# A gate product in blocks of two, and sums made by adding transfers, in a two-layer hybrid backbone

## The chip, the cores and the metric

The kernel runs on one core of one Trainium2 chip. The metric is the device time of one execution in microseconds. Engines are called as in the profile: PE (TensorE, the matmuls), DVE (VectorE), ACT (ScalarE), POOL (GpSimd), SP (SyncE, which here only issues transfers).

## What is computed

Two layers over 1024 latent tokens of width 1024, and 256 context tokens. Layer 0 has a convolution branch A and a recurrent branch B behind one input projection; layer 1 is a pooling mixer. Everything is float32. The part that the change touches is layer 0:

```python
shift, scale, gate = split(silu(c) @ mod_w[l] + mod_b[l], 3)
hx = rmsnorm(x, norm_g[l]) * (1 + scale) + shift
va, vg, ga, xb, gb = split(hx @ w_in)                  # each 1024 wide
u   = depthwise_conv(va * sigmoid(vg), conv_w, conv_b)     # 31 taps
y_a = silu(layernorm(u, ln_g, ln_b)) * silu(ga)
y_b = (scan_forward + scan_backward of xb's gated input) * silu(gb)
x   = x + gate * (concat(y_a, y_b) @ w_out)
```

Layer 1 needs its own shift and scale, which are `silu(c) @ mod_w[1]`.

## The kernel before

The state is held transposed: channels on 128 partitions, tokens along the row, so a 1024-channel tensor is 8 tiles of 128x1024, and each tile is worked in two halves of 512 tokens. A float32 product is made of three passes: each operand is split into a high part (a cast to fp32r) and a low part (the rest), and hi·hi, hi·lo and lo·hi are summed. `hh` and `hl` are the two parts of the 8 tiles of modulated tokens (h0h, h0l in the profile). One output tile of 128x512 thus takes 8 × 3 = 24 matmuls, each 128x128 by 128x512. A weight block is loaded as a 128x1024 tile (`wr_...`), cast on ACT (`wh_...`), and its low part made on POOL (`wl_...`) or DVE.

The order of the work is written out by hand. `on(engine, ...)` links each instruction of PE, DVE, ACT and POOL behind the one written before it on that engine, as long as `fixed[0]` holds, and SP issues its transfers in program order. The stages, with their times in the profile:

1. A prologue to about 62 us: folding of two layer-1 weights, modulations, the norm of the tokens (`xs` is the normalized token tile, `x_high` and `x_low` make hh and hl), then the first products to about 98 us.
2. Eight rounds, j = 0 to 7, of 42.47 us each. A round makes vg and va of channel block j (`u` = va·sigmoid(vg)), the next block's xb for the recurrence, and its gates. Meanwhile the recurrence of block j − 1 is finished: `rec_scan` on DVE for the two directions, `rec_sum`, which adds the directions on DVE, and a store to `yb_raw`. `raw_split` near the round's end casts the weights of the next round's vg (`wl_vg` on POOL). `fill(n)` puts n taps of the depthwise convolution on DVE between other work.
3. The products gb (to 490 us), the gating of branch B (`gated`: yb_raw is reloaded, multiplied, split; the low part `ybl` on POOL), and the B half of the output product, wob (490 to 579 us), whose results are added to x on POOL and stored (`wob_evict`, `x1_part`). The layernorm over channels needs sums over the 8 tiles of u: `ln_sums` adds them on DVE, `ln_mean` finishes the mean with matmuls by ones.
4. The product ga, 579 to 666 us: all 8 channel blocks × 2 halves × 24 matmuls. Under it lie the second part of the layernorm, the gating of u by silu(ga), and the splits of the result (`ya`) for the next product.
5. The A half of the output product, woa, from 666 us. It is already computed in blocks of two: with channel blocks and token halves as a 2 × 2 matrix of blocks on each side, seven products of sums of blocks take the place of eight (`BOPS` names the operands: four blocks and sums t1 to t4).
6. Folding for layer 1, to 790 us, and layer 1 to the end. The layer-1 modulation is made on DVE, by one multiply-and-sum over 512 elements for each of 16 tiles and 2 halves (`mod_halves`, L1386).

Of the kernel before, what the change touches and what calls it, by code (L numbers as in the profile page):

```python
# [15 lines left out]
P = 128  # L16
# [30 lines left out]

BOPS = ("b11", "t1", "t2", "b21", "t3", "b22", "t4")
# [3 lines left out]
def body(ctx, tc, xT, ctxT, cc, ccol, modT, modW, win, gw, wout, wu, grp, wg, wo1, small, edge, ident, outT):  # L52
    nc = tc.nc
    mult, add, sub = ALU.mult, ALU.add, ALU.subtract
# [13 lines left out]
    y_raw = [{n: dram.tile([P, 2 * S], F32, tag=f"y_{n}_{p}", name=f"y_{n}_{p}") for n in BOPS} for p in range(2)]  # L68
    x1_part = [dram.tile([P, S], F32, tag=f"x1_part{j}", name=f"x1_part{j}") for j in range(KT)]
# [227 lines left out]
    with ExitStack() as sctx:  # L297
# [133 lines left out]

        g_load(0)
# [107 lines left out]
        x_low(1)  # L540
        fold_all(5, 0, 0, 1)
# [14 lines left out]
        fold_copy(5, 1)  # L556
        w_load(7)
        fold_store(1)
        w_load(8, win[3 * KT])
# [54 lines left out]
        c_square(0)  # L614
        fold_copy(7, 1)
# [3 lines left out]
        w_load(10, win[0])  # L619
        for n in range(5, 8):  # L620
            fold_store(n)
# [74 lines left out]
    def raw_load(src, name):  # L696
        raw = wpool.tile([P, D], F32, tag="wr", name=f"wr_{name}")
        nc.sync.dma_start(raw, src)
        return raw

# [8 lines left out]


# [65 lines left out]
    ended, summed, spread_ = [0], [1], [0]  # L776
    NSPREAD = 5

    def ln_sums():
        for j in range(summed[0], ended[0]):  # L780
            for h in range(2):
                first = us[0][:, HALF[h]] if j == 1 else lnacc[h][:, :H]
                vec(nc.vector.tensor_tensor, out=lnacc[h][:, :H], in0=first, in1=us[j][:, HALF[h]], op=add)
        summed[0] = max(summed[0], ended[0])
# [16 lines left out]
    def at_rest():  # L801
        ln_sums()
        while spread_[0] < min(whole_[0], ended[0] + 2, NSPREAD):
            spread_sum()

# [14 lines left out]
    with ExitStack() as actx:  # L820
# [56 lines left out]
        def rec_sum(st):  # L877
            hs, hb = st[2][1], st[2][3]
            vec(nc.vector.tensor_tensor, out=hs[:, C:], in0=hs[:, C:], in1=hb[:, C:], op=add)
            nc.sync.dma_start(yb_raw[st[0]], hs[:, C:])  # L880
# [22 lines left out]
        for j in range(KT):  # L903
# [20 lines left out]
            if j:  # L924
                wva = raw_split(raw_load(win[j], f"va{j}"), f"va{j}")
            sg = [ttile(f"sg{j}_{h}") for h in range(2)]
# [42 lines left out]
            whole_[0] = j + 1  # L969
            if state is None:  # L970
# [39 lines left out]
            fill(19 if state is None else 6)  # L1010
# [7 lines left out]
        def gb_weights(j):  # L1018
            src, name = ((win[4 * KT + j], f"gb{j}") if j < KT else
                         (wout[j - KT, 1], f"wob{j - KT}") if j < 2 * KT else  # L1020
                         (win[2 * KT + (0, KT // 2)[j - 2 * KT]], f"ga{(0, KT // 2)[j - 2 * KT]}"))
            gws[j] = raw_split(raw_load(src, name), name)

        def gb_product(j, w):
            if j == 4:
                gps[j] = (lambda t: [t[:, h] for h in HALF])(wide(f"gb{j}"))
            else:
                gps[j] = [psum(f"gb{j}_{h}") for h in range(2)]
            for h in range(2):
                all_of(mm3_fixed(gps[j][h], w, (hh, hl), HALF[h]))  # L1030

        sbs = {}

        def gb_silu(j):
            sbs[j] = [ttile(f"sb{j}_{h}") for h in range(2)]
            for h in range(2):
                act(sbs[j][h], gps[j][h], AF.Silu)

        gb_product(1, w)
# [5 lines left out]
        gb_product(2, gws[2])  # L1045
# [6 lines left out]
        gb_product(3, gws[3])  # L1052
        fill(24)
        rec_scan(state, 0)
        raw = raw_load(win[4 * KT + 4], "gb4")
# [6 lines left out]
        rec_sum(state)  # L1062
        at_rest()

# [9 lines left out]
    m1p = hpool.tile([P, 2 * KT, 2], F32, name="m1p")  # L1074
# [6 lines left out]

    KH = KT // 2
# [30 lines left out]
    def wquad_steps(ops, src, name, ring, late=False, hold=None):  # L1113
# [14 lines left out]
        ops[1] = op(a11, 1)  # L1128
        if late:
# [88 lines left out]
    bh, bl = [], []  # L1218
    def gated(n, between):
        th, tl = d2tile(f"ybh{n}", F32R), d2tile(f"ybl{n}", F32R)  # L1220
        for h in range(2):
            y = vtile(f"yr{n}_{h}")
            nc.sync.dma_start(y, yb_raw[n][:, HALF[h]])
            v = sbs[n][h]
            vec(nc.vector.tensor_tensor, out=v, in0=y, in1=v, op=mult)
            cast(th[:, HALF[h]], v)
            gp(out=tl[:, HALF[h]], in0=v, in1=th[:, HALF[h]].bitcast(F32), op=sub)
            fill(between)
        bh.append(th)
        bl.append(tl)  # L1230

    gb_product(4, gws[4])
    gated(0, 3)
    gb_silu(2)
    gb_weights(5)
    gb_product(5, gws[5])
    gated(1, 3)
    for j in range(3, KT + 1):
        if j == 4:
            gb_weights(j + 2)  # L1240
        if j < KT:
            gb_silu(j)
        if 4 < j < KT - 1:
            gb_weights(j + 2)
        if 3 < j < KT - 2:
            gb_product(j + 2, gws[j + 2])
        gated(j - 1, (0, 0, 4, 5, 5, 3, 1, 0)[j - 1])
        if j == KT:
            gb_weights(KT + 1)
            fill(8)  # L1250
        ln_sums()


    def wob_evict(m, h):
# [1079 lines left out]
```

## Time and profile before

| | us |
|---|---|
| Median of 3 runs (lowest, highest) | 1268.86 (1266.57, 1268.94) |
| Profiled execution, span of the core | 1263.6 |
| Difference between the profiled span and the median | 5.3 |
| Time of a round (wl_vg at 159.16 to wl_vg at 201.63) | 42.47 |
| Product ga, first start to last | 578.9 to 666.2 |

"Span" is the time from the first to the last instruction in the trace. Busy shares are averages over the whole span. Lines like `L161 PE MATMUL ga<-h0h,wh_ga x96: 389/389/389, 601.1 to 665.7` give the engine, the operation, the tile written and the tiles read, the count, the shortest, median and longest duration in ns, and the first and last start. In the groups, the two numbers behind the bar are the busy time of the group in us and the mean duration in ns, and then the idle time before. In a timeline row the first number is the start, the second the duration. Almost all instructions of layer 0 carry the line of a helper (L670 before, L699 after), so groups are told apart by their tiles.

### The profile page before, as it was taken

Reading aid. Unit: us, or ns where it says so; the run is one execution under the profiler, and the core shown is the slowest. Engines: PE = TensorE matmul, PEld = TensorE weight load, DVE = VectorE, ACT = ScalarE, POOL = GpSimd, SP = SyncE. Lnnn points to the kernel's source line nnn. Section 1 sums busy time; section 2 is a strip of 40 time slices with the busy share of each in tenths; the row PEclk is TensorE's granted clock in tenths of the full one; section 3 lists DMA queues with packets and bytes.
Section 4 is the critical chain, followed back from the end, with each engine's and each line's share of the span. In section 5 each row is a group of like instructions: output and inputs, shape, how many; then the busy total and the mean of one; then the engine's idle time right before and its main releaser. Section 6 shows DMA issues by size and latency. Waiting matters only on the chain.

```text
span 1263.6 us, 16209 instructions
## 1 busy us (share of the span) xinstructions
PE 1249.8 (99%) x5866; PEld 1035.6 (82%) x5866; DVE 1139.3 (90%) x1746; ACT 653.8 (52%) x952; POOL 295.7 (23%) x176
## 2 busy tenths in 40 slices
PE   9999999999999999999999999999999999999997
PEld 7788888888888888888887878888888888888786
DVE  7799999999999999998978969999899987977975
ACT  8464566656666534237535445744343444644642
POOL 0015364436444547543210023000000000000002
PEclk9999999999999999999999999999999999999999
DMA  9970121112121233442436666344323334759723
GB/s 376 388 254 33 52 65 46 63 43 75 42 84 42 84 119 132 159 150 84 147 112 225 202 206 183 103 136 148 125 94 140 117 125 126 268 199 335 285 71 134
DMA packets 78705, 182.29 MB, mean 144 GB/s; under 512 B 7712, under 2 KB 23328, under 8 KB 78624
## 3 DMA queue, kind: packets, MB, share of 16 engines
q1 hardware_dynamic: 67328, 172.33, 39.8%
q10 hardware_dynamic: 11296, 8.92, 2.2%
q8 instruction: 46, 0.75, 0.2%
q14 instruction: 35, 0.29, 0.1%
HBM read 137.18 MB, written 44.04 MB: 143 GB/s over the span
## 4 chain that ended last, share of the span: by engine, by line
PE 70%; DVE 18%; DMA 7%; issue 2%; ACT 2%; POOL 1%; SPq 0%; POOLq 0%; ACTq 0%; DVEq 0%
PE wob L670 7%; DVE conv L670 5%; PE va L670 5%; PE xb L670 4%; PE vg L670 4%; DVE l L670 3%; PE fold L670 3%; PE g L670 3%; PE qb_v L1153 2%; PE ga L670 2%; PE qb_g L1156 2%; PE ga L161 2%; PE qb_v L1156 2%; PE qb_g L1155 2%; PE qb_g L1153 2%
## 5 line engine op out<-in xcount | busy, mean ns | idle before, releaser
L670 DVE SCALAR_TENSOR_TENSOR conv<-u,sm,conv 128x505 f32<-128x505 f32 (+6 forms) x224 | 153.6, 744 | 1.0
L2045 POOL TENSOR_TENSOR o<-x,rr 128x256 f32<-128x256 f32 (+1 forms) x10 | 9.2, 952 | 448.4 <-ACT rr L2045 448.4
L670 ACT ACTIVATE l<-g,sm 128x512 f32<-128x512 f32 (+1 forms) x96 | 58.7, 619 | 57.7 <-PE g L670 57.0
L670 POOL TENSOR_TENSOR l<-l,l 128x1280 f32<-128x1280 f32 x16 | 47.1, 2967 | 25.6 <-ACT l L670 15.1
L670 PE MATMUL gb<-h0h,wl_gb 128*128 128x512 f32 x128 | 49.9, 390 | 0.4 <-POOL wl_gb L670 0.4
L670 PE MATMUL va<-h0h,wl_va 128*128 128x512 f32 x128 | 49.9, 390 | 0.2 <-DVE wl_va L670 0.2
L98 ACT CAST wq_g<-wr_g 128x512 fp32r<-128x512 f32 x48 | 28.2, 621 | 41.9 <-DMA wr_g<-wg 15.6
L670 PE MATMUL gb<-h0l,wh_gb 128*128 128x512 f32 x128 | 49.8, 389 | 0.0
L670 PE MATMUL gb<-h0h,wh_gb 128*128 128x512 f32 x128 | 49.8, 389 | 0.0
L670 PE MATMUL va<-h0l,wh_va 128*128 128x512 f32 x128 | 49.8, 389 | 0.0
L670 PE MATMUL va<-h0h,wh_va 128*128 128x512 f32 x128 | 49.8, 389 | 0.0
L670 PE MATMUL wob<-ybl,wh_wob 128*128 128x512 f32 x128 | 49.8, 389 | 0.0
L670 PE MATMUL wob<-ybh,wl_wob 128*128 128x512 f32 x128 | 49.8, 389 | 0.0
L670 PE MATMUL wob<-ybh,wh_wob 128*128 128x512 f32 x128 | 49.8, 389 | 0.0
L670 DVE TENSOR_TENSOR_SCAN l<-l,l 128x256 f32<-128x256 f32 (+1 forms) x32 | 48.7, 1521 | 1.1
L670 DVE SCALAR_TENSOR_TENSOR conv<-cL,wsum,conv 128x506 f32<-128x506 f32 (+3 forms) x70 | 48.1, 745 | 0.2
L670 POOL TENSOR_TENSOR l<-l,uc 128x1280 f32<-128x1280 f32 x16 | 47.6, 2999 | 0.0
L98 ACT CAST wq_wo<-wr_wo 128x512 fp32r<-128x512 f32 x48 | 28.6, 620 | 35.5 <-DVE wr_wo L1134 12.4
L98 ACT CAST wq_v<-wr_v 128x512 fp32r<-128x512 f32 x48 | 28.1, 620 | 33.7 <-DMA wr_v<-wfold 16.6
L670 PE MATMUL xb<-h0l,wh_xb 128*128 128x512 f32 x112 | 43.8, 391 | 0.0
L670 PE MATMUL xb<-h0h,wh_xb 128*128 128x512 f32 x112 | 43.8, 391 | 0.0
L670 POOL TENSOR_TENSOR wl_xb<-wr_xb,wh_xb 128x1024 fp32r<-128x1024 f32 x7 | 16.8, 2407 | 114.5 <-ACT wh_xb L670 114.5
(680 smaller groups left out, 4362.5 us busy)
## 6 DMA issues: line engine op xcount, KB each, us to landing
modw<-modW SPq DMA_DIRECT2D x16, 512.0 KB, 10.2
mod<-modT SPq DMA_DIRECT2D x32, 256.0 KB, 3.4
wr_v<-wfold SPq DMA_DIRECT2D x16, 512.0 KB, 4.0
wr_g<-wg SPq DMA_DIRECT2D x16, 512.0 KB, 4.3
wr_wo<-wo SPq DMA_DIRECT2D x16, 512.0 KB, 4.1
mod<-modT SPq DMA_DIRECT2D x14, 512.0 KB, 4.5
y_b<-y SPq DMA_DIRECT2D x24, 256.0 KB, 3.5
y_t<-y SPq DMA_DIRECT2D x24, 256.0 KB, 3.1
```

The lines of the kernel that those rows point to most:

```text
L98: return (nc.scalar.copy(hi, src), eng.tensor_tensor(out=lo, in0=src, in1=hi.bitcast(F32), op=sub))
L161: mm(ps, hi[:, kc], xh[k][:, cols], start=(k == 0), stop=False)
L670: last[eng] = f(*args, **kw)
L1153: nc.tensor.matmul(ps, hi, xh[k], start=(first and k == 0), stop=False, skip_group_check=not first)
L1155: nc.tensor.matmul(ps, hi, xl[k], start=False, stop=False, skip_group_check=not first)
L1156: mm = nc.tensor.matmul(ps, lo, xh[k], start=False, stop=(k == KH - 1), skip_group_check=not first)
L2045: tail[eng] = f(*args, **kw)
```

## The change

The kernel is altered in these parts.

- **Gate product in blocks of two.** ga is made like woa, by seven products per pair of channel blocks (q = 0 to 3), in an order written as a table (`GORDER`). It no longer stands between wob and woa but begins before the second half of gb5 and ends before gb6, among the last taps of the convolution. After wob, woa follows at once. The norm's mean follows the last ga product, and its squares, root, scale and SiLU, the gating by ga and the splits of ya lie under gb6, gb7 and wob. silu(ga) is stored to DRAM and reloaded, and so is silu(gb) for blocks 0 to 5.
- **Token sums by transfers.** The seven products need sums of blocks of tokens. ACT negates half of each normalized tile (`x_out`), SP stores the tiles to `h_raw`, and in the rounds plain copies within DRAM and adding transfers (`plus`, issued by POOL, the destination is added to) make the sums t1 to t4.
- **Weight sums by transfers.** Sums of weight blocks (`wsums`) are made likewise in DRAM.
- **Direction sums by transfers.** `rec_sum` goes; the first direction is stored to yb_raw, the second added by a transfer.
- **Norm sums by transfers.** u0 to u4 are summed in DRAM (`ln_raw`), u5 and u6 added to the reloaded sum by transfers, u7 on DVE.
- **Residual.** x1_part is filled with x by copies in DRAM, and wob's results are added to it by transfers; POOL's additions go.
- **Layer-1 shift.** Half of the layer-1 modulation is made from rows of the weights in another layout (`modN`), scaled on ACT, summed by transfers and finished by 8 one-column matmuls in the folding stage.
- **Fill counts.** The numbers of taps placed between other work change.

The diff, cut to its core:

```diff
+GORDER = ([(0, p) for p in (1, 2, 5, 6, 3, 7)]
+          + [x for q in (1, 2, 3) for x in ((q, 1), (q - 1, 4), (q, 2), (q, 5), (q, 6), (q, 3), (q, 7))] + [(3, 4)])
...
+        def x_out(k):
+            v = xs[k][:, HALF[1 - k // KH]]
+            A.activation(v, v, AF.Identity, scale=-1.0)
+
+        def x_store(k):
+            load(h_raw[:, k * S : (k + 1) * S], xs[k])
...
         c_square(0)
+        for k in range(4, 8):
+            x_out(k)
         fold_copy(7, 1)
         c_square(1)
         cast(A, 9)
         low(9)
         w_load(10, win[0])
+        for k in range(2, 8):
+            x_store(k)
...
+    def plus(dst, src):
+        on("pool", nc.gpsimd.dma_start, dst, src, accum_op=add, max_dma_last_dim=8192)
...
+                if j < KT - 1:
+                    plus(lnacc[h][:, :H], us[j][:, HALF[h]])
+                else:
+                    vec(nc.vector.tensor_tensor, out=lnacc[h][:, :H], in0=lnacc[h][:, :H], in1=us[j][:, HALF[h]], op=add)
...
+    COPIES = {1: (("t1", h11), ("t3", h22)), 2: (("t2", h22), (0, a11)), 3: ((1, a21),),
+              4: ((2, 0), ("t4", "t2")), 7: ((3, 2),)}
+    ADDS = {1: (("t1", h12),), 2: (("t3", h12),), 3: (("t2", "t1"), (0, a21)), 4: ((1, a22),),
+            5: (("t4", h21), (2, a22)), 7: ((3, a12),)}
...
-        def rec_sum(st):
-            hs, hb = st[2][1], st[2][3]
-            vec(nc.vector.tensor_tensor, out=hs[:, C:], in0=hs[:, C:], in1=hb[:, C:], op=add)
-            nc.sync.dma_start(yb_raw[st[0]], hs[:, C:])
+        def rec_store(st, d):
+            latent = st[2][2 * d + 1][:, C:]
+            if d == 0:
+                nc.sync.dma_start(yb_raw[st[0]], latent)
+            else:
+                plus(yb_raw[st[0]], latent)
...
                 for d in range(2):
                     rec_scan(state, d)
-                rec_sum(state)
+                    rec_store(state, d)
+                sum_adds(j)
...
-                gates, roots = [e, f, r0, r1], [i1, i0]
+                gates, roots = [e, f, r0, r1], [i0, i1]
...
-            fill(19 if state is None else 6)
+            fill(19 if state is None else 6 if final else 8)
...
+    def ga_op(n):
+        if n >= len(GORDER):
+            return
+        t = wpool.tile([P, D], F32R, tag=("wh", "wl")[n % 2], name=f"wq_ga{n}")
+        hi, lo = ga_w[GORDER[n]] = [t[:, h] for h in HALF]
+        if GORDER[n][1] == 6:
+            act(hi, ga_src[n], AF.Identity, scale=-1.0)
+            vec(nc.vector.scalar_tensor_tensor, out=lo, in0=ga_src[n], scalar=-1.0, in1=plain(hi), op0=mult, op1=sub)
+        else:
+            cast(hi, ga_src[n])
+            gp(out=lo, in0=ga_src[n], in1=plain(hi), op=sub)
...
+    for n, (q, p) in enumerate(GORDER):
...
+        ga_product(q, p, ps, first, end)
...
+        if p == 3:
+            vtt(out=c, in0=c, in1=ga_part[q, "b"], op=add)
+        if p == 7:
+            a = ttile(f"gs{q}_1_1")
+            vtt(out=a, in0=b, in1=ga_part[q, "c"], op=add)
+        ln_sums()
+        fill([7, 2, 1, 1, 2, 3, 3, 4, 3, 4, 4, 3, 4, 3, 4, 3, 4, 4, 3, 4, 3, 4, 3, 4, 4, 2, 1, 0][n])
+        if n == 26:
+            ln_event("end")
+        if n == 27:
+            ln_event("mean")
+        ga_op(n + 3)
...
     def wob_evict(m, h):
-        v = ttile(f"wo_{m}_{h}")
-        act(v, wob_ps[m][h], AF.Identity, scale=m0[:, 0, 2 * KT + m : 2 * KT + m + 1])
-        t = vtile(f"xp{m}_{h}")
-        nc.sync.dma_start(t, xT[m][:, HALF[h]])
-        gp(out=t, in0=t, in1=v, op=add)
-        nc.sync.dma_start(x1_part[m][:, HALF[h]], t)
...
+        plus(x1_part[m][:, HALF[h]], v)
...
-        for h in range(2):
-            ga_product(j, gws[2 * KT + n], h)
-            if (n, h) == (0, 1):
-                ln_root(1, lnparts)
...
+    for n in range(KT):
+        mmo(mod_p[:, n : n + 1], mod_q[n // 4][:, n % 4 * P : (n % 4 + 1) * P], ones[:, 0:1], start=True, stop=True,
+            skip_group_check=True)
```

POOL's order at the end of round 5 before (l are the recurrence's buffers, uc the short convolution's result, wl_vg6 the low part of a weight). The two l products of the recurrence are followed at once by the next round's vg weights:

```order
L670 TENSOR_TENSOR l1_910<-l1_910,l4_913 128x1280
L670 TENSOR_TENSOR l3_912<-l3_912,l5_914 128x1280
L670 TENSOR_TENSOR wl_vg6_2942<-wr_vg6_2804,wh_vg6_2941 128x1024
L670 TENSOR_TENSOR l5_914<-l5_914,uc5_2500 128x1280
L670 TENSOR_TENSOR l2_911<-l2_911,uc5_2500 128x1280
```

The same place of round 5 after the change:

```order
L699 TENSOR_TENSOR l0_951<-l0_951,l2_953 128x1280
L699 TENSOR_TENSOR l1_952<-l1_952,l4_955 128x1280
L699 DMA yb_raw4_89<-l1_952 128x1024
L699 DMA h_t4_114<-h_raw_110 512x1x512
L699 DMA wsum2_117<-win 512x512
L699 TENSOR_TENSOR wl_vg6_3006<-wr_vg6_2870,wh_vg6_3005 128x1024
L699 TENSOR_TENSOR l4_955<-l4_955,uc5_2560 128x1280
L699 TENSOR_TENSOR l5_956<-l5_956,uc5_2560 128x1280
```

Three transfers now stand on POOL between the recurrence's products and the next weights; the first of them waits for DVE's second scan.

ACT's order in the prologue before, around the squares of the context tokens (csq, from cx) and the last folded weight (fo):

```order
L119 ACTIVATE csq_0_2_797<-cx_0_784 128x256
L119 ACTIVATE csq_0_3_800<-cx_0_784 128x256
L119 COPY fo_7_759<-fold_7_1_771 128x4x128
L119 ACTIVATE csq_1_0_804<-cx_1_786 128x256
L119 ACTIVATE csq_1_1_807<-cx_1_786 128x256
```

And after the change:

```order
L131 ACTIVATE csq_0_2_829<-cx_0_816 128x256
L131 ACTIVATE csq_0_3_832<-cx_0_816 128x256
L131 ACTIVATE x_4_267<-x_4_267 128x512
L131 ACTIVATE x_5_273<-x_5_273 128x512
L131 ACTIVATE x_6_275<-x_6_275 128x512
L131 ACTIVATE x_7_277<-x_7_277 128x512
L131 COPY fo_7_791<-fold_7_1_803 128x4x128
L131 ACTIVATE csq_1_0_840<-cx_1_818 128x256
```

Four negations of half tiles stand between the first context tile's squares and the second's.

More of the change, by code (lines that the diff above doesn't have):

```diff
@@ L1232, in body @@
[L1232 to L1251, printed above, removed]
@@ new lines, in body, with yb_tiles, gate_mult @@
+    bh, bl = [None] * KT, [None] * KT
+    def yb_tiles(n):
+        th, tl = d2tile(f"ybh{n}", F32R), d2tile(f"ybl{n}", F32R)
+        nc.sync.dma_start(plain(tl), yb_raw[n])
+        if n < NB:
+            nc.sync.dma_start(plain(th), sb_raw[n])
+        bh[n], bl[n] = th, tl
+    gate_out = {}
+    def gate_mult(n):
+        gate_out[n] = [ttile(f"gated{n}_{h}") for h in range(2)]
+        for t, h in zip(gate_out[n], HALF):
+            vtt(out=t, in0=plain(bl[n][:, h]), in1=plain(bh[n][:, h]), op=mult)
+            cast(bh[n][:, h], t)
@@ L1263, in body, with gate_low @@
+    def gate_low(n):
+        for t, h in zip(gate_out[n], HALF):
+            vtt(out=bl[n][:, h], in0=t, in1=plain(bh[n][:, h]), op=sub)
     lnmu, lnsq = {}, {}
@@ L1396, in body, with ln_event @@
-    mods = mod_halves()
+    lnparts = [None, None]
+    def ln_event(e):
+        if e == "end":
+            while ended[0] < KT:
+                fill(1)
+            ln_sums()
+            for q in range(2):
+                hi = vpool.tile([P, H], F32R, tag="v", name=f"mh_mu{q}")
+                lo = tpool.tile([P, H], F32R, tag="t", name=f"ml_mu{q}")
+                cast(hi, lnacc[q][:, :H])
+                vtt(out=lo, in0=lnacc[q][:, :H], in1=plain(hi), op=sub)
+                lnparts[q] = hi, lo
+        elif e == "mean":
+            for q in range(2):
+                ln_mean(q, lnparts[q])
+        elif e[:2] == "sq":
+            q, part = int(e[2]), e[3:]
+            for j in range(KH) if part == "a" else range(KH, KT):
+                ln_square(j, q)
+                if j > 1:
+                    ln_add(j - 2, q)
+            if part == "b":
+                for j in (KT - 2, KT - 1):
+                    ln_add(j, q)
+                lnparts[q] = mean_parts(lnacc[q][:, :H], f"ln{q}")
+        elif e[:4] == "root":
+            ln_root(int(e[4]), lnparts[int(e[4])])
+        elif e[:5] == "scale":
+            ln_scale(int(e[5]))
+        elif e[:4] == "silu":
+            q = int(e[4])
+            for j in (0, KH, 1, KH + 1, 2, KH + 2, 3, KH + 3):
+                ln_silu(j, q)
@@ new lines, in body, with chain_split, wo_op, t3_low @@
+    wo_tiles = {}
+    def chain_split(hi, lo, src):
+        cast(hi, src)
+        vtt(out=lo, in0=src, in1=plain(hi), op=sub)
+    def wo_op(n, v):
+        if n not in wo_tiles:
+            wo_tiles[n] = ring_w(f"wq_woa0_{n}")
+        t = wo_tiles[n]
+        chain_split(t[:, HALF[0]], t[:, HALF[1]], v)
+    def t3_low():
+        low = parted[1]
+        for hi, lo, v in zip(*ya["t3"], kept["t3"]):
+            with tc.issue_after(low.ins):
+                low = nc.vector.tensor_tensor(out=lo, in0=v, in1=plain(hi), op=sub)
+        return low
@@ L1447, in split_kept @@
+    mods = mod_halves()
+    def wo_weights(m):
+        return wquad([wout[m + i, 0] for i in range(2)], f"woa{m}", ring_w, **(dict(mid=last_split, first=t3_low) if m == 2 else {}))
+    w0 = tuple(wo_tiles[n] for n in range(1, 8))
     def split_kept(name):
```

544 lines of the change are left out of this document (391 added, 153 removed).

## The prediction

> **What bounds the kernel now.** I read the page first, then the list of what TensorE (PE) waited for, then the stages the change touches: the gate product as a tile, a round of the main loop as a timeline, and the prologue.
>
> ```profile
> span 1263.6 us, 16209 instructions
> PE 1249.8 (99%) x5866; PEld 1035.6 (82%) x5866; DVE 1139.3 (90%) x1746; ACT 653.8 (52%) x952; POOL 295.7 (23%) x176
> DMA  9970121112121233442436666344323334759723
> PE 70%; DVE 18%; DMA 7%; issue 2%; ACT 2%; POOL 1%; SPq 0%; POOLq 0%; ACTq 0%; DVEq 0%
> PE fin_ms L2045 <- DVE dg L2045: 1.2, 1, 1.2
> PE gb L670 <- POOL wl_gb L670: 0.4, 1, 0.4
> ```
>
> PE is busy for 99% of the span, the chain of waits runs over it for 70%, and its longest single wait anywhere is 1.2 us. So PE bounds almost every stage, and time comes off where matmuls come off, as long as VectorE (DVE, 90%) and the producers of the operands keep up. The DMA row has nines only in the first two slices of 31.6 us and in one late one.
>
> What a removed matmul is worth is not what its row says it lasts:
>
> ```profile
> L161 PE MATMUL ga<-h0h,wh_ga x96: 389/389/389, 601.1 to 665.7; 128*128 128x512 f32 x96
> L163 PE MATMUL ga<-h0h,wl_ga x96: 389/389/389, 601.6 to 666.2; 128*128 128x512 f32 x96
> 579.00:666.00 87.00, 87.00 (x386) 71.98 (x385) 75.68 (x124) 46.95 (x72) 20.26 (x9) 1.00 0.35 114
> ```
>
> The 288 matmuls of lines 161 to 163 start between 601.1 and 666.2, one every 65.1/287 = 0.2268 us, while each lasts 0.389: they overlap. The stretch 579 to 666 says the same (386 matmuls in 87 us, 0.2254), at a granted clock of 1.00 and with DVE busy 75.68 of 87.
>
> **The change, part by part.**
>
> Gate product. 8 row blocks × 2 halves × 24 = 384 matmuls become 28 products × 12 = 336. 48 × 0.2268 = **−10.9 us**. The matmuls that go are of the same 128x512 form, so this term is firm.
>
> DVE's work. These groups go, wholly or in part:
>
> ```profile
> L670 DVE TENSOR_TENSOR l<-l,l 128x1024 f32<-128x1024 f32 x7 | 8.6, 1225 | 0.2
> L1386 DVE SCALAR_TENSOR_TENSOR mod<-mod,cH 128x512 f32<-128x512 f32 x32 | 27.7, 887 | 5.0 <-ACT cH L257 3.1 <-DMA mod<-modT 1.8
> L670 DVE TENSOR_TENSOR lnsum<-lnsum,u 128x512 f32<-128x512 f32 x8 | 5.1, 684 | 0.0
> L670 POOL TENSOR_TENSOR ybl<-sb,ybh 128x512 fp32r<-128x512 f32 x16 | 22.4, 1411 | 29.2 <-DMA yb_raw<-l 15.4 <-ACT ybh L670 13.8
> L670 DVE SCALAR_TENSOR_TENSOR conv<-u,sm,conv 128x505 f32<-128x505 f32 (+6 forms) x224 | 153.6, 744 | 1.0
> ```
>
> Off DVE go the direction sums, 8 × 1.225 = 9.8; 16 of the 32 modulation products, 16 × 0.887 = 14.2; and 12 of 14 norm sums, 12 × 0.684 = 8.2. On come, all half-tile operations of 0.68 to 0.74 like the rows above: 16 low parts of the gated B branch that POOL did (10.9), 8 splits of h sums (5.9), 4 low parts of the negated weights (3.0) and 8 corner additions (5.5). That is −32.2 + 25.3 = −7 us on DVE, whose cover is PE either way, so I cost the exchange itself at nothing.
>
> The gate product now stands among the last convolution taps. In its steady state seven products take 7 × 12 × 0.2268 = 19.05 us of PE, and the code gives DVE in that time about 25 taps (153.6/224 = 0.686 each, 17.2) and two or three half-tile operations (1.9): 19.1. This is balanced to the percent, with operands prepared three products (8.2 us) ahead. If each tap cost its full 0.744, DVE would be 1.45 late per seven products, 5.8 over 28; if the taps overlap as in their row, nothing. I take 0.5, since the row measured the same taps in a row.
>
> The cover that is lost: before, the gate product's 87 us lay between the B half of the output product (wob) and the A half (woa), with the norm's second half, the gating and the splits of A under it, and DVE had 11.3 us free there. Now these lie under the last gb halves and wob, 20 halves of 24 matmuls, 108.9 us of PE. Counting the new order by the rows above gives DVE about 95 us there, 87%. Nothing is late by this count; the first that would be is the split of A's last blocks behind wob. Bounds 0 and 5.9 (eight half-tile operations at 0.74, the splits of one block); I take 0.
>
> Prologue. Eight half tiles are negated on ScalarE (ACT) and 8 stores of 512 KB added.
>
> ```profile
> 67.06 1.02 ACT L119 ACTIVATE csq<-cx 128x256 f32<-128x256 f32 x3
> 67.98 0.57 ACT L119 COPY fo<-fold 128x512 f32<-128x512 f32 x1
> 68.45 1.34 ACT L119 ACTIVATE csq<-cx 128x256 f32<-128x256 f32 x4
> 69.69 1.04 ACT L119 CAST wh<-wr 128x1024 fp32r<-128x1024 f32 x1
> 71.07 1.22 DVE L119 TENSOR_TENSOR wl<-wr,wh 128x1024 fp32r<-128x1024 f32 x1
> 85.34 1.22 DVE L670 SCALAR_TENSOR_TENSOR mod<-mod,cL 128x1024 f32<-128x1024 f32 x1
> 86.48 1.22 DVE L670 TENSOR_TENSOR wl_va<-wr,wh_va 128x1024 fp32r<-128x1024 f32 x1
> L670 PE MATMUL va<-h0h,wl_va 128*128 128x512 f32 x128 | 49.9, 390 | 0.2 <-DVE wl_va L670 0.2
> 20.00:73.00 53.00, 52.40 (x399) 39.78 (x398) 42.71 (x66) 33.99 (x53) 0.00 (x0) 1.00 1.02 375
> L130 SPq DMA_DIRECT2D mod<-modT x6: 376/453/945, 69.0 to 72.3; - x6
> DMA to landing us min/median/max: 5.1/8.0/9.6
> ```
>
> Four of the negations go between the csq row of 67.06 and the fo row of 67.98, where ACT has no gap until the cast ends at 70.73. At 0.57 each (the fo row) they push that cast, DVE's low part behind it and then DVE's unbroken queue by 2.3 us, down to wl_va, for which PE already waited 0.2. The other way to the same place is DMA: the share there is 1.02 at 375 GB/s, and six of the stores (3.1 MB) stand ahead of the modulation rows, whose landing (the last two rows, issued from 69.0 on) took up to 9.6: 69.0 + 9.6 + 8.4 = 87.0 against the DVE row at 85.34, 1.7 late. Both shift the same DVE queue and so overlap. Bounds 0 and 4.0; I take **+2.3**.
>
> The rounds. Seven times the direction sum leaves DVE and becomes a plain store plus an adding transfer issued by POOL, and POOL also issues one or two more adding transfers (of tokens, of weights) before its next weight split:
>
> ```profile
> 194.46 3.08 DVE L670 TENSOR_TENSOR_SCAN l<-l,l 128x256 f32<-128x256 f32 x2
> 197.57 1.23 DVE L670 TENSOR_TENSOR l<-l,l 128x1024 f32<-128x1024 f32 x1
> 159.16 2.41 POOL L670 TENSOR_TENSOR wl_vg<-wr_vg,wh_vg 128x1024 fp32r<-128x1024 f32 x1 [14.35 <-DVE conv L670]
> 201.63 2.40 POOL L670 TENSOR_TENSOR wl_vg<-wr_vg,wh_vg 128x1024 fp32r<-128x1024 f32 x1 [14.37 <-DVE u L670]
> 161.97 0.39 PE L670 MATMUL vg<-h0h,wl_vg 128*128 128x512 f32 x1
> 205.31 2.61 ACT L670 ACTIVATE l<-l,chalf 128x1280 f32<-128x1280 f32 x2
> L880 SPq DMA_DIRECT2D yb_raw<-l x8: 320/327/327, 156.3 to 443.6; - x8
> yb_raw<-l SPq DMA_DIRECT2D x8, 512.0 KB, 2.6
> ```
>
> The first adding transfer waits for the scan that ends at 197.57; wl_vg starts at 201.63. POOL was idle there, so 4.06 us cover its new issues. Behind wl_vg PE has 0.40 more (one round earlier wl_vg ends at 161.57 and its first reader starts at 161.97). The cover is therefore 4.46 us per round, for two issues in rounds 1, 2, 4 and 7 and three in 3 and 5. No row of before has a transfer issued by POOL. The bounds of one issue: 0.33 us (SP's store of the same 512 KB) and 2.40 (POOL itself passing over a 128x1024 tile). An issue moves no data through its engine, so I go by the lower row, but not all the way: 0.9 each as an estimate (the geometric mean of the two), 2.7 at most against 4.46, hence **0**. At 2.40, two are 0.34 late and three 2.74: 4 × 0.34 + 2 × 2.74 = 6.8 in all. What could be late next is ACT's row at 205.31, which overwrites the buffer that is being added: its second half, at 206.6, leaves 9.0 us for a landing that takes a plain store 2.6.
>
> By the Trainium skill, "DMA: Bandwidth & Descriptors", section "SWDGE vs HWDGE vs iDMA", such an adding transfer must go by GpSimd, where software computes its descriptors, one pair for each piece, while SP's are made by hardware; by this rule the price lies nearer POOL's row than I put it, and the rounds would cost up to 6.8 instead of 0. No run so far shows which.
>
> The rest. DRAM copies, reloads and adding transfers of the evictions lie where the DMA row shows 1 to 7 tenths; SP issues some 62 more at 0.33, 20 us over a span in which it isn't waited for. The layer-1 shift by 8 one-column products in the fold stage lies between 0 and 8 × 0.2268 = 1.8; I take 0.5, because DVE's small operations behind them are fewer than those removed.
>
> Sum: −10.9 + 2.3 + 0.5 + 0 + 0.5 = −7.6, so a span of 1256.0. The profiled span of 1263.6 stands 5.3 below the median of the runs, 1268.86, so **1261.3 us**.
>
> **Rivals.**
>
> All hidden. ACT's shift dies in DVE's queue and the taps overlap: −10.9 and 0.4 for the fold, 1258.4. For it speaks that PE waited for wl_va only 0.2; against it that this wait exists, so that there is no slack at all.
>
> POOL pays for its issues, by bytes. This is the case on the other side. If the price is p per 512 KB, the sums of 1 MB cost 2p: two issues in a round are 3p, three are 5p, against 4.46 of cover. Late: 4 × (3p − 4.46) + 2 × (5p − 4.46). At p = 1.6 this is 1.4 + 7.1 = 8.5, which gives 1270; at p = 2.4 (POOL's row) 11.0 + 15.1 = 26, 1287. Slower begins at p = 1.7. Between, at a flat 2.40 an issue (6.8), the result is 1268.1, no change. Against it: SP's 0.33 for any size of one tile; for it: POOL takes 2.4 where DVE takes 1.22 for the same split.
>
> The A branch is late at woa. DVE has 87% by count in a chain of dependent steps (mean, squares, root, scale, SiLU, gating, splits), and a late link leaves PE waiting at woa's first products. By the upper bound, 1261.3 + 5.9 − 0.5 (the taps' term, which is in it) = 1266.7, and less if the link is late by less. Before, the 87 us of gate product absorbed this.
>
> The removed matmuls count in full. By their busy rows 48 × 0.389 = 18.7 would go, 1253.5. The spacing of the starts speaks against it. The Trainium skill's "Trainium Kernel Development and Optimization", under "Performance Expectations", calls matmul busy time a bad metric because matmuls are pipelined; the trace agrees (0.389 against 0.2268).
>
> **How the numbers follow.** No change means within 0.2%, 2.5 us, about what a measurement of this kernel can tell: 1266.3 to 1271.4. Chances: my sum 0.40 (own range 1259 to 1264), all hidden 0.21, matmuls in full 0.02, A late 0.13 (half of it late by less and still faster), POOL flat 0.11, POOL by bytes 0.13. Faster 0.40 + 0.21 + 0.02 + 0.07 = 0.70; no change 0.06 + 0.11 = 0.17; slower 0.13. The range 1256 to 1270 leaves out the full count below and most of the by-bytes case above, some 0.17.
>
> **What would show it.** Right: the gate product at 0.2268 per matmul with no PE wait over 1 us from gb to woa; wl_vg in rounds 3 and 5 starting no later than before relative to the scan's end; one wait of about 2 us of PE for wl_va near 88 us; rounds of 42.47 us as before (159.16 to 201.63). Wrong: wl_vg late in the rounds with three adding transfers, and vg waiting for POOL; PE waiting for DVE at the norm's mean or for a split at woa; or weights in the first rounds landing late because of the stores.

## The result: 1.6% slower, and where the time went

The changed kernel takes 1287.42 us (median of 4 runs, 1285.12 to 1291.87) against 1267.98 for the kernel before on the same chip, 1.0156 of it (95% interval 1.0140 to 1.0172). The forecast was 1261.3 with a range to 1270: wrong in sign. The profiled execution spans 1290.1 us, 26.5 more than before's 1263.6; the account below is made against these two. This trace is of the slowest of the four executions, so the 26.5 is more than the 19.4 between the medians, and the profiled execution of e3 below (granted clock 0.65, 1791.11 us) is left out throughout. The page of the changed kernel, the first lines and the chain's shares:

```profile
span 1290.1 us, 16419 instructions
PE 1252.9 (97%) x5834; PEld 1031.4 (80%) x5834; DVE 1138.7 (88%) x1711; ACT 687.4 (53%) x1013; POOL 314.9 (24%) x211
DMA  9992364545542695885796866244233334759713
PE 30%; DVE 3%; DMA 2%; issue 1%; ACT 1%; POOL 0%; POOLq 0%; ACTq 0%; DVEq 0%
```

The list of transfers, three rows (count, size of one, median us from issue to landing):

```profile
yb_raw<-l POOLq DMA_DIRECT2D x8, 512.0 KB, 5.1
wsum<-win POOLq DMA_DIRECT2D x4, 1024.0 KB, 16.0
gl<-ga_raw SPq DMA_DIRECT2D x16, 256.0 KB, 7.5
```

PE has fewer matmuls and is busy 3.1 us longer over a longer span: 97% in place of 99%. The chain's shares can't be set against those of before: they sum to 37% of the span, since the chain could be followed back no further, where before they summed to 100%. DVE's busy time is 1138.7, as before (1139.3), where my count took 7 us off it. In the rounds (fourth to fourteenth slice) the digits of the DMA row rise from 0 to 2 before to 2 to 6, and an adding transfer of 1 MB takes 16.0 us to land, one of 512 KB 5.1. What PE waited for, the largest first:

```profile
PE qb_woa L1240 <- ACT qb_woa L1847: 4.1, 1, 4.1
PE g L699 <- ACT l L699: 3.9, 1, 3.9
PE mu L699 <- DVE ml_mu L699: 2.0, 1, 2.0
PE ms_ln L699 <- ACT mh_ln L699: 1.9, 2, 1.0
PE ms_c L152 <- DVE ssqc L131: 1.8, 1, 1.8
PE qac_wo L1243 <- DVE wq_wo L111: 1.4, 1, 1.4
PE qb_ga L699 <- DVE gs L699: 1.2, 2, 1.0
```

Before, no wait was longer than 1.2. Now there are waits in the rounds (g is the gate matmul of the recurrence), at the norm (mu and ms_ln are its mean and mean square) and in woa. To place the loss I take three first starts from PE's timeline, before:

```profile
396.03 0.40 PE L670 MATMUL gb<-h0h,wh_gb 128*128 128x512 f32 x1
666.42 0.39 PE L1153 MATMUL qa_woa<-ya_b11h,wq_woa 128*128 128x512 f32 x1
789.78 0.39 PE L1153 MATMUL qa_v<-x_b11h,wq_v 128*128 128x512 f32 x1
```

and after:

```profile
407.32 0.40 PE L699 MATMUL gb<-h0h,wh_gb 128*128 128x512 f32 x1
680.33 0.39 PE L1240 MATMUL qa_woa<-ya_b11h,wq_woa 128*128 128x512 f32 x1
812.81 0.39 PE L1240 MATMUL qa_v<-x_b11h,wq_v 128*128 128x512 f32 x1
```

Their differences are the stages. In brackets stands what PE lost there: first its waits (all idle times over 0.15 us), then the rest of the stage beyond 0.2257 us per 512 columns of its matmuls. In the last stage this rest holds small matmuls and the end without matmuls, in both kernels alike; from after's third stage the one-column rows (1.7 us) are taken out. The versions e1, e5, e15 and e16 are experiments below.

| us | start to gb | gb to woa | woa to layer 1 | layer 1 to end |
|---|---|---|---|---|
| before | 396.0 (2.5 + 3.0) | 270.4 (0.5 + 1.7) | 123.4 (1.3 + 1.1) | 473.8 (2.7 + 15.2) |
| after | 407.3 (10.6 + 6.3) | 273.0 (8.7 + 6.9) | 132.5 (5.8 + 4.0) | 477.3 (4.7 + 16.7) |
| e1 | 398.8 | 273.0 | 133.2 | 478.9 |
| e5 | 399.5 | 270.3 | 127.7 | 476.8 |
| e15 | 399.1 | 271.3 | 127.8 | 476.1 |
| e16 | 398.9 | 271.0 | 139.2 | 476.3 |

11.3 us are lost ahead of gb. From gb to woa 48 matmuls are gone (1193 starts before, 1145 after), worth 10.9, and yet the stage is 2.6 longer: 13.5 were given back, 8.3 as waits and 5.2 as matmuls that start further apart. Another 9.1 go between woa and layer 1, and 3.5 in layer 1.

### The profile page after: what moved, and what is told of

Read it like the earlier page. It is cut to its first block, busy times and chain, and to the rows that moved or that the text cites. A ratio compares the mean times of both kernels' runs of the same rounds, so it can differ in the third digit from the quotient of the medians.

```text
span 1290.1 us, 16419 instructions
## 1 busy us (share of the span) xinstructions
PE 1252.9 (97%) x5834; PEld 1031.4 (80%) x5834; DVE 1138.7 (88%) x1711; ACT 687.4 (53%) x1013; POOL 314.9 (24%) x211
## 5 line engine op out<-in xcount | busy, mean ns | idle before, releaser
L110 ACT CAST wq_wo<-wr_wo 128x512 fp32r<-128x512 f32 x48 | 28.6, 619 | 38.6 <-DMA wr_wo<-wo 13.5
L699 PE MATMUL vg<-h0h,wl_vg 128*128 128x512 f32 x112 | 43.8, 391 | 1.4 <-POOL wl_vg L699 1.4
L699 PE MATMUL xb<-h0h,wl_xb 128*128 128x512 f32 x112 | 44.1, 393 | 0.0
```

What stands on the lines that cost most here:

```text
L110: return (nc.scalar.copy(hi, src), eng.tensor_tensor(out=lo, in0=src, in1=hi.bitcast(F32), op=sub))
L699: last[eng] = f(*args, **kw)
```

## The experiments

The versions that change one place of the changed kernel start either from it or from e1; e8, e9 and e13 start from the kernel before. Each ratio is against the kernel before on the chip of that run.

**The changed kernel once more**, unaltered, on another chip.

> The changed kernel once more, unaltered, as the measure for the runs beside it: 1287, within 3 us either way.

1290.55 us against 1266.74, 1.0190 (1.0175 to 1.0205). The loss is no accident of one chip. In this trace gb starts at 404.69, 2.6 earlier than in after; the wait for g is 1.8 and vg waits 3.3 in three places: the same late weights, divided otherwise.

**The rounds: who is late.** The prediction weighed POOL's issues. They are cheap. POOL's timeline of after, end of round 5:

```profile
337.42 0.89 POOL L699 DMA_DIRECT2D yb_raw<-l  x1 [12.26 <-DVE l L699]
338.01 1.53 POOL L699 DMA_DIRECT2D h_t<-h_raw  x1
338.65 1.94 POOL L699 DMA_DIRECT2D wsum<-win  x1
339.31 3.69 POOL L699 TENSOR_TENSOR wl_vg<-wr_vg,wh_vg 128x1024 fp32r<-128x1024 f32 x1
```

Three issues take 339.31 − 337.42 = 1.89 us, 0.63 each, two of them for 1 MB. (The split behind them lasts 3.69, where POOL's rows of before have 2.40, and vg waits 1.0 for it.) But round 4 (wl_vg at 247.64 to wl_vg at 296.58) lasts 48.9 us in place of 42.5. The timeline there, with the two adding transfers that POOL issued at the end of round 3, and SP's issues:

```profile
244.42 1.19 POOL L699 DMA_DIRECT2D h_t<-h_t  x1
244.96 1.69 POOL L699 DMA_DIRECT2D wsum<-win  x1
...
256.36 0.49 SPq L863 DMA_DIRECT2D h_t<-h_t  x1
256.95 0.52 SPq L727 DMA_DIRECT2D wr_xb<-win  x1
266.11 0.48 SPq L863 DMA_DIRECT2D wsum<-wsum  x1
266.68 0.53 SPq L1024 DMA_DIRECT2D wr_gw<-gw  x1
```

SP works in order. Each copy of L863 (`sum_copies`) reads a sum that an adding transfer is still making, so SP stands at it until that has landed: 256.36 − 244.42 = 11.9 us for the tokens, 266.11 − 244.96 = 21.2 for the weights. The loads of wr_xb and wr_gw, which depend on none of this, stand behind them. ACT and PE then, in the same timeline (in brackets the wait and its releaser):

```profile
266.33 1.05 ACT L699 CAST wh_xb<-wr_xb 128x1024 fp32r<-128x1024 f32 x1 [4.66 <-DMA wr_xb<-win]
272.37 0.62 ACT L699 CAST wh_gw<-wr_gw 128x512 fp32r<-128x512 f32 x1 [4.98 <-DMA wr_gw<-gw]
...
283.18 0.58 PE L699 MATMUL g<-uh,wh_gw 128*128 128x256 f32 x1 [3.92 <-ACT l L699]
```

e1 issues the copies later in the round, behind the load of the next vg:

```diff
                 wva = raw_split(raw_load(win[j], f"va{j}"), f"va{j}")
-                sum_copies(j)
...
             raw = raw_load(win[4 * KT + 1] if final else win[KT + j + 1], name)
+            if j:
+                sum_copies(j)
```

> The changed kernel, with the plain copies of a round (h_t, wsum within DRAM) put on SP's queue behind the load of the next vg weights instead of ahead of the load of the next xb weights. All adding transfers stay as they are. Theory A (SP's queue stands still behind a copy that waits for an adding transfer to land, and the weights behind it come late): round 4 goes from 48.9 back to 42.5 us, the 3.9 us wait of PE for the gates goes, and with it the slow matmuls after it; 1287.4 - 6.4 = 1281. Rival B (POOL's issues, or the traffic of the sums, cost the rounds their time): nothing of that has moved, round 4 stays over 47 us and the time at 1286 to 1288.

1284.44 us, 1.0123 (1.0102 to 1.0143), its span 1283.9. Round 4 takes 42.48 again, the wait for g is gone, and gb starts at 398.78, 8.5 earlier than in after and 5.9 earlier than in e0. No engine's work was changed, only SP's order: the queue was the cause. Against after's span later stages gave 2.3 of it back.

**The direction sums alone**, in the kernel before:

```diff
-                rec_sum(state)
+                    rec_store(state, d)
...
-                gates, roots = [e, f, r0, r1], [i1, i0]
+                gates, roots = [e, f, r0, r1], [i0, i1]
```

> The kernel before, with one part of the change alone: the direction sums (DVE, 8 of 1.2 us) replaced by a plain store and an adding transfer issued by POOL in each round. Theory A (POOL's issue is cheap, 0.9 us by the trace, and hidden): no wait of PE in the rounds, the round stays 42.47 us, the time within 2 us of before, DVE's convolution gets ahead by 8 us by the rounds' end. Rival (an adding transfer holds back POOL's weight splits or ACT's next use of the buffer): the rounds lengthen by 0.4 us or more each, 3 us or more slower than before.

1269.01 us, 1.0019 (1.0007 to 1.0031). The trace is of its fastest execution: the span is 1263.4 (before 1263.6), gb starts at 396.25 (396.03), and PE waits for nothing in the rounds. One adding transfer a round is hidden but for the 0.2% of the median, which this trace does not place, and the 9.8 us of sums that it takes off DVE gain nothing.

**The prologue alone**: `x_out` and `x_store` at the change's places, in the kernel before.

> The kernel before, with one part of the change alone: the eight negations on ACT and the eight stores to h_raw in the prologue, at the places where the change has them (nothing reads h_raw). Theory A (ACT's order and the stores delay DVE's full queue up to wl_va): PE waits 1.8 us at ms_c and about 1 at va, 2 to 4 us slower than before. Rival (the prologue's waits come from something else in the change): the same time as before within 1 us.

1270.23 us, 1.0019 (1.0005 to 1.0032); gb starts 2.0 late, the span is 2.2 longer. Its waits hold one new row:

```profile
PE ms_c L141 <- DVE ssqc L120: 1.8, 1, 1.8
```

The size is the predicted 2.3, but PE pays ahead of wl_va: at the context tokens' mean square, whose squares ACT delivers behind the negations. e2 therefore issues the negations earlier, among the last splits of the tokens, in the changed kernel:

```diff
+        for k in range(4, 7):
+            x_out(k)
         for k in range(4, 8):
...
+            if k == 5:
+                x_out(7)
...
         c_square(0)
-        for k in range(4, 8):
-            x_out(k)
```

> The changed kernel, with ACT's four negations of the upper half tiles put ahead of the last scaling loop, where ACT waits for DVE 1.95 us, instead of between the squares of the context tokens. Theory A (ACT's order pushes DVE's queue): PE's waits for ms_c (1.8) and for wl_va (1.15) go, 1287.4 - 2.9 = 1284.5. Rival B (the stores to h_raw ahead of the modulation rows make DVE late): the store order is unchanged, so wl_va still starts near 89 us and the wait at va stays, at most 1 us gained.

1292.43 us, 1.0192 (1.0167 to 1.0216): no gain. The wait for ms_c went, and PE waits 5.4 us for wl_va instead. DVE's timeline of e2:

```profile
89.43 3.35 DVE L701 TENSOR_TENSOR wl_va<-wr,wh_va 128x1024 fp32r<-128x1024 f32 x1
```

In after wl_va takes 1.22 (from 89.26) and POOL's next split follows it; here POOL's split of wr_xb runs at the same time (from 89.06) and DVE's row lasts 3.35. DVE's row ends 1.08 behind POOL's (92.78 and 91.70), nearly its own length, as if it had stood until POOL was done. That the two hold each other up is read from one pair of rows and not shown.

**The A branch at woa.** PE's longest wait stands at woa's third product. DVE's timeline of after, ahead of it:

```profile
670.38 0.69 DVE L699 TENSOR_TENSOR u<-u,gl 128x512 f32<-128x512 f32 x1 [1.69 <-DMA gl<-ga_raw]
672.45 0.69 DVE L699 TENSOR_TENSOR u<-u,gl 128x512 f32<-128x512 f32 x1 [1.38 <-DMA gl<-ga_raw]
...
687.13 0.69 DVE L699 TENSOR_TENSOR yat<-u,u 128x512 f32<-128x512 f32 x1 [1.46 <-DMA x_part<-wo]
```

DVE does not lack time, it waits: for silu(ga) to come back from DRAM, and for buffers that an adding transfer of wob's results still reads. e5 is e1 without the reload; it leaves out the gating by silu(ga) and multiplies u by itself:

```diff
-            vtt(out=v, in0=v, in1=gl_loaded.pop(0), op=mult)
-            gl_load()
+            vtt(out=v, in0=v, in1=v, op=mult)
```

> The changed kernel with the copies later in the round, and with the 16 reloads of silu(ga) left out: each half tile of u is multiplied by itself instead, so DVE does as many operations on as much data, and 4 MB of loads go. It does not compute silu(ga)'s gating. Theory A (the A branch is late at woa because its chain on DVE waits for late loads): DVE's idle time under wob falls by 4 us or more, PE's wait of 4 us at woa's second product goes with the slow matmuls behind it, 5 to 7 us under the copies-later kernel's 1284.4: 1278. Rival C (DVE has too much work there, whatever the loads do): the wait at woa keeps 3 us or more, at most 2 us gained.

1277.70 us, 1.0090 (1.0075 to 1.0105); the changed kernel took 12.9 more on this chip (e0). The wait of 4.1 at qb_woa is gone with the same work on DVE. Against e1, on another chip, the span is 9.6 shorter, 5.5 of it between woa and layer 1. e5 also takes 4 MB of loads out of the queues, so it does not separate the wait for the reload from its traffic. Moving DVE's work instead helped nothing. e3 moves the four differences of sum t3 (`yat3`) behind two more splits in the changed kernel; e14 does this with e1, e2 and a reload of yb_raw that is issued behind the load of gb6's weights:

```diff
-    for i in range(KH):
-        kept["t3"][i], v = (vtile if i < 2 else ttile)(f"yat3_{i}"), kept["t3"][i]
-        vtt(out=kept["t3"][i], in0=us[KH + i][:, HALF[1]], in1=v, op=sub)
     vtt(out=a11, in0=a21, in1=a11, op=sub)
...
         chain_split(*[v[i] for v in ya["b22"]], kept["b22"][i])
+    for i in range(KH):
+        ...
```

> The changed kernel, with the four differences for t3 (DVE, the last of which waited 1.5 us for an adding transfer to land) moved behind the weight operands 6, 2, 3 and the b22 splits at the start of the output product's A half. Theory A (one late link in DVE's order): PE's wait of 4.1 us before the second operand product falls under 1.5, the slow matmuls behind it go too, 4 to 6 us less: 1282 to 1283. Rival B (DVE as a whole is late there, since the cover is gone): the wait comes back at a later product of the same block and the time stays within 1.5 us of 1287.

> Four orders at once: copies later, negations earlier, t3 differences later, and the reloads of yb_raw and sb_raw behind the load of gb6's weights (which landed after 8.2 us behind four other loads, and held ACT's queue ahead of the norm's mean). No work is removed. Theory A (the loss is waits from queue order, and they add up): 6.4 + 2.9 + 5 + 4 (waits of 2.0 and 0.7 at the mean, and slow matmuls after) = 18 less, 1269, level with before. Rival B (the same lateness turns up elsewhere because DVE, or the transfers' traffic, is the real limit): less than 9 us gained, over 1278.

e3: 1293.57 (the median of five), 1.0202 (1.0177 to 1.0227). e14: 1289.43, 1.0158 (1.0134 to 1.0181), with this among its waits:

```profile
PE qc_woa L1243 <- DVE x L701: 3.6, 1, 3.6
```

The wait moved on by one product and stayed: the whole chain behind the norm is late, not one link at its end.

e16 is e1 with the layer-1 shift made on DVE again, so the loads, ACT scalings and adding transfers of `modN` under wob are gone:

```diff
-    mod_fold()
...
-                for n in (k, k + 1):
+                for n in (k, k + 1, KT + k, KT + k + 1):
```

> The changed kernel with the copies later, and with one part of the change undone: layer 1's shift is made on DVE again (16 operations of 0.89 us under woa), so eight loads of 512 KB, six adding transfers, their ACT scalings under wob and the eight one-column matmuls go. Theory A (ACT and the transfers under wob are what delays the A branch): the wait at woa's second product falls under 2 us, and the time by 3 us or more under 1284.4. Rival (DVE's work in the woa stage is worth more): the wait at woa stays and DVE's 14 us make PE wait later, 1285 or more.

1289.24, 1.0167 (1.0154 to 1.0180). qb_woa no longer waits for ACT, so that work (loads, scalings and adding transfers, which e16 does not separate) had been part of A's delay. But DVE now multiplies under woa, and PE's largest wait is 10.4 for the weights wq_woa. ACT's timeline shows what they stand behind:

```profile
730.47 0.63 ACT L269 ACTIVATE cH<-cH 128x512 f32<-128x512 f32 x1 [11.96 <-DMA cH<-cc]
```

ACT stands 12 us at `cH`, whose load SP issues only at 725.13, and PE's weights come behind it. In this version the shift costs there too; in the kernel before it was made there as well, and PE's waits in the whole stage were 1.3.

**The norm.** e6 (from e1) makes the mean and the squares' products by ones later, and loads gb6's weights ahead of the reload of yb_raw, to see whether PE only arrives too early:

```diff
-        if n == 27:
-            ln_event("mean")
...
-        for e in {2: ('sq0a',), 3: ('sq0b',), 5: ('sq1a',), 6: ('root0', 'sq1b'), 7: ('scale0',), ...
+        for e in {0: ('mean',), 2: ('sq0a',), 3: ('sq0b',), 5: ('sq1a',), 6: ('sq1b',), 7: ('root0',), ...
```

> The changed kernel with the copies later, gb6's weights loaded ahead of the reloads of yb_raw, and PE's matmuls by ones moved back in its order: the mean's from right after the gate product to behind the first half of gb6, and the two of the variance by one half product (5.4 us) each; scale, SiLU follow them. No work is removed. Theory A (PE stands still because these small matmuls come ahead of work that doesn't depend on them): the waits at mu (1.6 and 0.7), at ms_ln (2.1, 0.5 and more) and the slow matmuls after them go, 6 us under 1284.4: 1278. Rival C (the chain behind them is what is late, and it ends later still): woa waits 3 to 6 us longer, and 1283 or more is measured.

1295.11, 1.0225 (1.0211 to 1.0240), where e1 has 1.0123. The waits for the operands of mu and ms_ln went, these came:

```profile
PE wob L699 <- ACT wh_wob L699: 6.6, 2, 6.3
PE qb_woa L1241 <- ACT qb_woa L1845: 3.7, 1, 3.7
```

What hangs on the mean is as urgent as PE's own work. e15 (from e5) takes the opposite way: the matmuls of mean and squares read a constant tile, so they need not wait for DVE's sums (the norm's statistics are left out):

```diff
     def mean(ps, parts):
-        for n, v in enumerate(parts):
-            on("pe", nc.tensor.matmul, ps, ones_r, v, start=(n == 0), stop=(n == 1))
+        for n in range(2):
+            on("pe", nc.tensor.matmul, ps, ones_r, flat, start=(n == 0), stop=(n == 1))
```

> The kernel without the reloads of silu(ga) and with the copies later (1277.7), in which the eight matmuls by ones of the layernorm read a tile of constants that is ready long before, instead of the sums. All work of DVE and ACT stays; mean and variance are constants, so it does not compute the norm. Theory A (PE stands behind the norm's sums at mu and ms_ln, since these matmuls come too early in its order for a late DVE): the waits there (1.8 at mu, 2.4 at ms_ln) go, and the chain behind them starts earlier, 4 to 6 us less, 1272 to 1274. Rival C (DVE's and ACT's work in these stages is late in itself): the waits move to the weights' casts or to woa, less than 2 us gained.

1277.77, 1.0080 (1.0067 to 1.0092), the same as e5. The waits changed their releaser and stayed:

```profile
PE ms_ln L699 <- DVE lnsum L699: 3.0, 1, 3.0
PE mu L699 <- ACT gs L699: 2.3, 1, 2.3
```

The operands are constant, so what is left to wait for is the PSUM bank: ACT's eviction of the last gate sum and DVE's last sum of the squares end these waits, and both read from PSUM. Operand or bank, the chain behind the norm is the limit.

**DVE under the gate product.** e10 (from e1) leaves out four taps each of the last convolution blocks, 12 in all; e11 is e10 with e5's edit and without the negations (h_raw is filled by copies of the raw tokens in round 0):

```diff
-        for i, n in enumerate([n for n in range(NT) if n not in (7, 8)]):
+        for i, n in enumerate([n for n in range(NT) if n not in (7, 8)][: -4 if j > 4 else None]):
```

> The changed kernel with the copies later, and 12 taps of the convolution left out (4 in each of blocks 5, 6 and 7), 8 us of DVE's work ahead of the norm's mean. It does not compute the full convolution. Theory A (DVE has no idle time from the rounds to the mean, and PE waits for it there): PE's waits for gs (1.0 and 0.9) and at mu (1.6 and 0.7) go, 3 to 6 us under the copies-later kernel's 1284.4: 1280. Rival (these waits come from the order, not from DVE's amount of work): they stay, 1283 or more.

> The changed kernel with four loads taken off at once: copies later; silu(ga) not reloaded (u multiplied by itself); the 12 taps left out; no negations and no stores to h_raw in the prologue (h_raw is filled from x by copies in DRAM in the first round instead). It does not compute the reference. Theory A (the gate product's 10.9 us are there, and the loss is the sum of these four lates): 1284.4 - 6.7 - 4 - 3 = 1271, with 6 us of it still lost at the variance and woa. Rival (the time lies elsewhere): over 1275.

e10: 1286.31, 1.0145 (1.0116 to 1.0174); e11: 1283.69, 1.0127 (1.0098 to 1.0156), where e5 has 1.0090. Both fill slots by count, so with fewer taps everything behind shifted: the mean's wait went, and `qb_ga` waited 2.9 for the low part of a token sum. In e11 the copies themselves made PE wait in round 1 (1.4 for g, 1.1 for vg). Inconclusive on what the taps cost; the sum of "all mended" that I expected of e11 wasn't reached.

**Slow matmuls behind a wait.** The rest in the stage table asks whether a wait costs more than itself. e13 is the kernel before with a wait put into round 4, by 13 idle copies on ACT; nothing else differs, no transfer is added:

```diff
+            if j == 4:
+                junk = ttile("junk")
+                for _ in range(13):
+                    act(junk, us[0][:, HALF[0]], AF.Identity)
```

> The kernel before, with 13 extra copies of a half tile on ACT in round 4, ahead of the cast of va's weights (7.2 us on ACT, of which the round hides 2.6): one wait of PE of about 4.5 us and nothing else. Theory A (a wait of PE of 2 us or more is followed by some 3.5 us of matmuls at half pace): the span is longer by the wait and 1.5 to 2.5 us more, 6 to 7 us in all. Rival (the slow matmuls in the changed kernel's trace come from its transfers): the span is longer by the wait alone, 4.5 us.

1274.36, 1.0056 (1.0036 to 1.0077). PE's timeline:

```profile
260.62 0.50 PE L670 MATMUL va<-h0h,wh_va 128*128 128x512 f32 x1 [2.34 <-ACT wh_va L670]
...
263.06 0.79 PE L670 MATMUL va<-h0h,wl_va 128*128 128x512 f32 x1 [1.70 <-POOL wl_va L670]
263.65 0.63 PE L670 MATMUL va<-h0h,wh_va 128*128 128x512 f32 x1
264.08 0.63 PE L670 MATMUL va<-h0l,wh_va 128*128 128x512 f32 x1
...
268.74 0.40 PE L670 MATMUL va<-h0h,wh_va 128*128 128x512 f32 x1
```

Two waits, 4.04 us together, and gb starts 8.0 late (404.06 against 396.03). Behind them twelve matmuls stand 0.43 apart (263.65 to 264.08) in place of 0.227 and last 0.63 in place of 0.39: 12 × 0.2 = 2.4. With 0.9 more at the first matmuls behind the two waits, 7.3 of the 8.0 are accounted for. The granted clock is 0.50 from 261.86 to 268.69, where before it is 1.00. Transfers can't be the cause, since e13 has none more than before: the wait is.

## Why the prediction was wrong, by its own steps

**Gate product, −10.9: right, and given back.** 48 matmuls are gone and the others keep their spacing (the first row of the windows below has 319 starts in 71.00 us, one every 0.2226). "Matmuls in full" is out.

**Prologue, +2.3: right in size** (2.0 to 2.2 in e9), at ms_c, not at wl_va alone.

**The rounds, 0: the step that failed first; 5.9 to 8.5 by e1.** It asked only what POOL's issues cost, and by POOL the answer held: 0.63 an issue against the 0.9 taken and bounds of 0.33 and 2.40. "POOL pays by bytes" fell with it: that its 1287 is the time measured is coincidence, since the issues of 1 MB cost no more than that of 512 KB. The rule of the Trainium skill, "DMA: Bandwidth & Descriptors", section "SWDGE vs HWDGE vs iDMA", that software on GpSimd makes these descriptors may hold, but the price of it is 0.6 us, not the 2.4 that I let it stand for. The step named SP's queue only by the price of an issue (62 × 0.33) and did not ask what each copy on it waits for. The order table shown ahead of it puts the adds at a round's end; the copies that read their sums, and the loads behind those copies on SP, had to be followed too. The copies with their sources stand in the diff (`COPIES`, `ADDS`).

**Taps under the gate product, +0.5: mis-sized.** DVE's fullness was counted rightly, and I chose the low end of 0 to 5.8. The windows of after:

```profile
407.00:478.00 71.00, 70.98 (x319) 58.63 (x318) 70.16 (x87) 34.29 (x43) 37.49 (x20) 1.00 0.70 198
478.00:552.00 74.00, 71.87 (x314) 58.32 (x313) 71.65 (x108) 35.13 (x63) 36.49 (x27) 1.00 0.71 225
...
588.00:678.00 90.00, 87.00 (x378) 70.35 (x377) 73.37 (x99) 60.39 (x87) 35.47 (x27) 1.00 0.81 206
678.00:733.00 55.00, 50.23 (x212) 40.06 (x211) 47.24 (x85) 25.76 (x46) 2.58 (x3) 0.97 0.72 225
```

The columns are the stretch, its length, and the busy time of PE, weight loads, DVE, ACT and POOL with their instructions, then the granted clock, the DMA share and GB/s. DVE is busy 70.16 of 71.00 and 71.65 of 74.00. Three waits of the product (0.94, 1.04 and 0.88) make 2.9. ACT ended the first of them and DVE the other two; e10 did not show what the taps themselves cost, so that these waits come from DVE's load is argued, not shown.

**Cover lost, 0 (bounds 0 and 5.9): the largest term that failed.** "A late at woa" was the right rival, placed rightly and priced too low. I counted DVE's load, 87%, and it was lower: 73.37 of 90.00 in the third row. But the stage is a chain (mean, squares, root, scale, SiLU, reload, gating, splits), whose links wait for ACT and for transfers of 5 to 8 us, and no count of an engine's work shows that. From gb to woa the waits at mean, squares and operands and what follows them make the rest of the 13.5; at woa come 4.1 more and their slow matmuls. e5 shows the share of one transfer in it, e15 and e14 that mending one link hands the wait to the next.

**Fold stage, +0.5.** Of woa to layer 1's +9.1, waits are 4.5 and wider spacing 2.9; the eight one-column products stand as 16 rows from 777.42 to 779.12, 1.7, near the upper bound of 1.8.

**Not in the sum at all: the slow matmuls.** Over the whole span, waits rose from 7.0 to 29.8 (+22.8) and the rest from 21.0 to 33.8 (+12.8). Up to layer 1 PE was busy for 11.7 us at a granted clock of 0.50, where before it was 1.00; at half pace this is 5.9 of the 12.8. Every wait was priced at its own length.

Open: layer 1's +3.5 (its waits rose by 2.0, the largest 1.4 at qac_wo), and how e5's 12.9 us of lost PE time between gb and woa, spread over the product's three waits, the mean and the squares, could be won back. No version here beats the kernel before; the best complete one is e1.

## What to carry to other kernels

When work is moved to transfers, follow for each transfer who waits for its landing, on which in-order queue, and what independent load stands behind that; the price of its issue is the small part. When a long stretch of PE work is removed, the chain of dependent steps that lay under it must be laid out with its latencies (each reload from DRAM 5 to 8 us here), not with its engines' busy shares. And a PE wait of 3.6 us or more is priced at its length plus some 1.7, one of 1.6 to 3 at that in about half the cases (the last section has the counts).

## What the hardware showed that was not expected

A wait makes the next matmuls slow. In after, behind the wait at woa:

```profile
690.13 0.50 PE L1240 MATMUL qb_woa<-ya_t2h,wq_woa 128*128 128x512 f32 x1 [4.10 <-ACT qb_woa L1847]
...
690.99 0.63 PE L1240 MATMUL qb_woa<-ya_t2h,wq_woa 128*128 128x512 f32 x1
691.41 0.63 PE L1242 MATMUL qb_woa<-ya_t2l,wq_woa 128*128 128x512 f32 x1
```

The spacing is 0.42 to 0.43 for seven matmuls, some 1.7 us lost beyond the wait, and the granted clock of the stretch 678 to 733 is 0.97 (the last row of the windows above), where the other three have 1.00. Over the traces of all these kernels (rounds to layer 1): behind each of the nine waits of 3.6 us and more, 5 to 12 matmuls came at 0.42 to 0.43; of seventeen single waits between 1.6 and 3.1 (none of 0.6 or more within 3 us of them), nine did this; of the single waits from 0.9 to 1.57, none, but two short ones close together (0.81 and 0.69 in e5) did.

The granted clock says where. In after it is 0.50 from 281.25 to 288.08, from 564.55 to 567.97 and from 690.85 to 694.26, in before nowhere from 5 to 1257 us. In each of the fifteen traces used here all its changes lie on one grid of steps of 3.413 us. Cut along these grids, from 90 to 1250 us, the traces have 23 steps at full clock in which PE was idle for 1.77 us or more, and behind each the clock was 0.50 in the next step. Behind the some 5000 steps with 1.49 us idle or less it never was, and behind the ten between, four times. So where a wait falls counts as well as its length: the wait of 3.01 in e15 is cut by the grid (1.44 and 1.57 us idle in the two steps) and was followed by no slow matmul, while one of 1.68 there lies within one step and was.

The Trainium skill's "TensorE: Matmul & The Clock Gate", Part 1, describes a gate that halves the clock after an idle window of about 3.4 us and opens it after as long a busy one, with 426.7 ns as the slow spacing of 512 columns. The spacing and the length of the window agree (0.427 and 3.413 us), and so does the page's statement that the window runs free of the kernel. That a whole idle window is needed doesn't: about half an idle one was enough.
